# Buffer counts of the gate stage: a second PSUM bank for the gates' matmuls, one bank fewer for transposes, seven one-hot buffers for four

## The chip, the cores and the metric

The kernel runs on one core of one Trainium2 chip. The metric is the device time of one execution in microseconds (us), the median of several runs. Lower is better.

## The reference, cut to what matters

One decoder block over 1024 tokens of width 1024, in float32. A projection feeds sliding-window attention and a short gated convolution; their output is projected, added to the input and normalised (h1). Then comes a mixture of single-neuron experts:

```
q  = h @ w_pq                        # per token 8 heads, two halves of 128
s1, s2 = q[..., :128] @ keys1.T, q[..., 128:] @ keys2.T
v1, i1 = top_k(s1, 16); v2, i2 = top_k(s2, 16)
sc, pos = top_k(v1[:, None] + v2[None, :], 16)
e  = i1[pos // 16] * 128 + i2[pos % 16]   # 16 of 16384 experts per head
g  = softmax(sc)
a  = gelu(u_experts[e] . h)               # 128 experts per token
out = sum_k g * a * v_experts[e]
```

and a second residual and normalisation.

## The kernel before, in words

The 1024 tokens are eight blocks of 128. For the expert stage they are handled in two ways. The blocks 2 to 5 (`DENSE`, L43) are computed densely: every expert's product with every token, by large matmuls, each masked by a gate that is zero for an expert not chosen. The blocks 0, 1, 6 and 7 (`ROWS`, L44) are gathered: for each of the 128 choices of a block, an indirect DMA fetches one row of 1024 floats per token.

**First stage (L207 to L678).** It goes over four groups of two blocks. `project` (L389) does one chunk of 128 output columns: a weight load on SP's queue and eight matmuls into the pool `pm`. The transposes and attention scores, the attention output and the products with the sub keys (L417, L442, L447, L459, L488, L492, L507, L544, L560, L583) all rotate through the pool `pt`, tag `tp`. `keys_of` (L574) takes the top 16 of each head's scores on VectorE. Each `project` also advances two side jobs. One is `side`, the generator `chosen` of the group before (L593), which runs `product_keys` (L301) and, for a dense block, `gates_of_all` (L232). The other is the gathered rows (`advance_rows`, L203).

**The gates (`gates_of_all`).** For eight tokens at a time VectorE builds three one-hot tiles of 128x1024 halfs, `o1` (L280), `oh` and `ol` (L285), all in the tag `hot`, which has four buffers. For each four of these tokens TensorE does eight matmuls (L291, L292) into one tile of the pool `pk`, which is one bank, and ScalarE evicts it in two halves (L295) to the two `st` tiles (tag `st`, two buffers). After 32 tokens both `st` tiles go to memory over SP's queue (L299, 1 MB each). A block is 32 such four-token tiles; the four dense blocks are 128.

**The gathered rows (`all_gathered`, L187).** One generator, in this order: the dot products of block 0 and of block 1 with u rows (`weights_of`, L150, one VectorE instruction a row, L159), the sum of block 0's v rows (`summed_on_pe`, L174), the sum of block 1's (`summed`, L165, one VectorE instruction a row, L170), then blocks 6 and 7 with `weights_of` and `summed`. `summed_on_pe` makes a diagonal tile on ScalarE (L180) and adds the row with two matmuls (L182) into the two banks of the pool `pg`; the profile has four matmul records a row. All rows share five buffers (`NGATHER`), and each gather is issued from POOL's queue (L141).

**Second stage (L681 to L802).** `up` and `down` stream all experts' weights over SP's queue and do the dense matmuls (L709, L741) into a pool of six banks that takes over the banks of `pk`, `pm` and `pt`. Its SBUF tiles too lie where those of the first stage lay. It begins with the reload of h (L691) and reads the gates back (L712). `advance` (L773) places the gathered rows among its units. It ends with `finish` (L754) and the second normalisation.

**Order.** Program order is a priority only: the kernel is built with `schedule_with_timeline_sim=True`, and a planner moves each engine's instructions past each other by its own simulated times and by when buffers come free. On the chip each engine then runs its list in that written order. The matmuls of `summed_on_pe` stand in program order in the second stage and are executed, by the trace, among the last gates of the first.

Of the kernel before, what the change touches and what calls it, by code (L numbers as in the profile page):

```python
# [13 lines left out]
F32 = mybir.dt.float32  # L14
F32R = mybir.dt.float32r
F16 = mybir.dt.float16
# [6 lines left out]
PS = bass.MemoryType.PSUM  # L23
DR = bass.MemoryType.DRAM

P = 128
# [25 lines left out]
OT = 8  # L52
# [25 lines left out]
def block_kernel(ctx: ExitStack, tc: tile.TileContext, d, out):  # L78
# [128 lines left out]
    with ExitStack() as s1:  # L207
        pa = s1.enter_context(tc.tile_pool(name="pa", bufs=1))
        gb = s1.enter_context(tc.tile_pool(name="gb", bufs=1))
        p1 = s1.enter_context(tc.tile_pool(name="p1", bufs=1))  # L210
        p2 = s1.enter_context(tc.tile_pool(name="p2", bufs=1))
        pk = s1.enter_context(tc.tile_pool(name="pk", bufs=1, space=PS))
        pm = s1.enter_context(tc.tile_pool(name="pm", bufs=2, space=PS))
        pt = s1.enter_context(tc.tile_pool(name="pt", bufs=3, space=PS))

        bias = p1.tile([P, 26], F32, name="bias")
        nc.sync.dma_start(bias, d["bias"])
# [14 lines left out]
        def gates_of_all(tb, e1, e2, g):  # L232


            f3 = gb.tile([P, 3, P], F32, name="f3", tag="hot", bufs=4)
            ei = gb.tile([P, P], I32, name="ei")
            V.tensor_copy(f3[:, 0], e1.rearrange("p h k -> p (h k)"))
            V.tensor_copy(ei, e2.rearrange("p h k -> p (h k)"))
            V.tensor_scalar(ei, ei, 7, None, op0=ALU.bitwise_and)
            V.tensor_copy(f3[:, 2], ei)  # L240
            V.tensor_tensor(f3[:, 1], e2.rearrange("p h k -> p (h k)"), f3[:, 2], op=ALU.subtract)
            tp = pk.tile([P, 4, P], F32, name="pk")
            for i in range(3):
                nc.tensor.transpose(tp[:, i], f3[:, i], ident)
            nc.tensor.transpose(tp[:, 3], g.rearrange("p h k -> p (h k)"), ident)
            iT = gb.tile([P, 5, P], F16, name="iT", bufs=2)
            act(iT[:, 0:3], tp[:, 0:3], AF.Copy)
            act(iT[:, 3], tp[:, 3], AF.Copy, scale=GSCALE)
            V.scalar_tensor_tensor(iT[:, 4], tp[:, 3], GSCALE, iT[:, 3], op0=ALU.mult, op1=ALU.subtract)
            i1w = gb.tile([P, P, OT], F16, name="i1w")  # L250
            act(i1w, tp[:, 0, :, None].to_broadcast([P, P, OT]), AF.Copy)

            def wide(o, i, n, step, t0):
                wshp = [P, n, HB // OT, OT]
                V.tensor_tensor(o.rearrange("p n (a t) -> p n a t", t=OT),
                                iT[:, i, t0:t0 + HB].rearrange("p (a t) -> p a t", t=OT)[:, None].to_broadcast(wshp),
                                keys[:, 0:n * step:step, None, :].to_broadcast(wshp), op=ALU.is_equal)

            shp = [P, P, OT]
            shr = [P, OT, P // OT, OT]  # L260
            for t0 in range(0, P, TG):
                if t0 % HB == 0:
                    da = gb.tile([P, 16, HB], F16, name="da")
                    wide(da, 1, 16, 8, t0)
                    db = gb.tile([P, 3, 8, HB], F16, name="db")
                    wide(db[:, 0], 2, 8, 1, t0)
                    for i in (1, 2):
                        V.tensor_tensor(db[:, i], db[:, 0], iT[:, 2 + i, None, t0:t0 + HB].to_broadcast([P, 8, HB]),
                                        op=ALU.mult)
                st = [gb.tile([P, NC // 2, TG], F32, name="st", bufs=2) for _ in range(2)]  # L270
                for t1 in range(t0, t0 + TG, OT):
                    ts = slice(t1, t1 + OT)
                    td = slice(t1 % HB, t1 % HB + OT)

                    def mk(name):
                        return gb.tile(shp, F16, name=name, tag="hot", bufs=4)

                    o1 = gb.tile([P, OT, P], F16, name="o1", tag="hot", bufs=4)
                    oh, ol = mk("oh"), mk("ol")
                    V.tensor_tensor(o1.rearrange("p t (a b) -> p t a b", b=OT),  # L280
                                    i1w[:, ts, None, :].to_broadcast(shr),
                                    row.rearrange("p (a b) -> p a b", b=OT)[:, None].to_broadcast(shr),
                                    op=ALU.is_equal)
                    for o, i in ((oh, 1), (ol, 2)):
                        V.tensor_tensor(o.rearrange("p (a b) t -> p a b t", b=8),  # L285
                                        da[:, :, None, td].to_broadcast([P, 16, 8, OT]),
                                        db[:, i, None, :, td].to_broadcast([P, 16, 8, OT]), op=ALU.mult)
                    for t2 in range(0, OT, 4):
                        ps = pk.tile([P, 4, P], F32, name="pk")
                        for t in range(4):  # L290
                            nc.tensor.matmul(ps[:, t], oh[:, :, t2 + t], o1[:, t2 + t], start=True, stop=False)  # L291
                            nc.tensor.matmul(ps[:, t], ol[:, :, t2 + t], o1[:, t2 + t], start=False, stop=True)  # L292
                        tt = t1 - t0 + t2
                        for z in range(2):
                            act(st[z][:, :, tt:tt + 4].rearrange("p n t -> p t n"),  # L295
                                ps[:, :, z * 64:(z + 1) * 64], AF.Copy, scale=1.0 / GSCALE)
                        yield
                for z in range(2):
                    nc.sync.dma_start(gd[((tb - D0) * P + t0) // TG, :, z * 64:(z + 1) * 64], st[z])  # L299

        def product_keys(tb, v16, i16):  # L301
# [61 lines left out]
            if tb in ROWS:  # L363
                ef = tk.tile([P, NH, TOPK], F32, name="ef")
                V.scalar_tensor_tensor(ef, e1, 128.0, e2, op0=ALU.mult, op1=ALU.add)
                ix = keep.tile([P, NH * TOPK], I32, name=f"ix{tb}")
                V.tensor_copy(ix, ef.rearrange("p h k -> p (h k)"))
                idx[tb] = ix
            else:
                yield from gates_of_all(tb, e1, e2, g)  # L370
# [469 lines left out]
```

## Time and profile before

| | us |
|---|---|
| median of 3 runs | 2766.03 |
| lowest and highest run | 2765.49, 2771.6 |
| the profiled execution | 2761.45 |
| its span, first to last instruction | 2759.6 |
| TensorE matmuls busy | 2476.9 (90%) |
| VectorE busy | 2156.7 (78%) |
| POOL busy | 1378.8 (50%) |
| ScalarE busy | 842.6 (31%) |

The span is cut at about 940 us (last projection), 1225 us (last gate), 1265 us (first dense matmul) and 2665 us (last dense matmul). PE is TensorE, PEld its weight load, DVE VectorE, ACT ScalarE; SPq is SP's DMA queue. A busy PE is not PE at its peak, since ends of matmuls are modelled.

### The profile page before, as it was taken

The page shows a single profiled execution, that of the slowest core. Times are in us where ns is not written, and L with a number is a line of the kernel's source. Part 1 is how long each engine was busy: PE and PEld are TensorE (multiplying, and loading weights), DVE is VectorE, ACT ScalarE, POOL GpSimd, SP SyncE. Part 2 cuts the span into 40 slices and gives each one's busy share as a digit, 9 for nine tenths or more (in the row PEclk, how much of TensorE's full clock was granted, in tenths as well). Part 3 has the DMA queues.
Part 4 walks back from the last instruction along what each step waited for, and adds up shares of the span by engine and source line. Part 5 has one row for each costly group of instructions (what it writes and reads, how often), then busy time and mean ns, then how long its engine had stood idle before and what let it go on. Part 6 is the DMA issues. An engine that isn't in the chain of part 4 may idle for free. (4 is left out here: it accounts for less than half of the span.)

```text
span 2759.6 us, 34442 instructions
## 1 busy us (share of the span) xinstructions
PE 2476.9 (90%) x11544; PEld 1992.3 (72%) x11544; DVE 2156.7 (78%) x4829; ACT 842.6 (31%) x1434; POOL 1378.8 (50%) x1233
## 2 busy tenths in 40 slices
PE   8999699779876999966999999999999999999960
PEld 7888588668765744435888888888888888888850
DVE  2158889999999844238888788888888888888898
ACT  2123122242433444343323332232322323232211
POOL 1001533443343244435666666666676666766663
PEclk9899799789977999987999999999999999999985
DMA  6345999899989588889999999999999999999997
GB/s 202 98 156 182 353 376 336 311 360 338 342 322 321 173 298 300 293 284 345 342 348 334 339 358 335 357 333 350 340 341 347 340 346 339 346 352 337 339 317 270
DMA packets 293905, 862.29 MB, mean 312 GB/s; under 512 B 25824, under 2 KB 97760, under 8 KB 289504
## 3 DMA queue, kind: packets, MB, share of 16 engines
q0 software_dynamic: 150480, 548.47, 54.4%
q1 hardware_dynamic: 143248, 311.62, 32.8%
q8 instruction: 91, 1.49, 0.2%
q14 instruction: 86, 0.70, 0.1%
HBM read 815.95 MB, written 44.04 MB: 312 GB/s over the span
## 5 line engine op out<-in xcount | busy, mean ns | idle before, releaser
L141 POOL DMA_INDIRECT row<-in_u,ix x512 | 526.0, 1027 | 625.0 <-DVE row L159 234.9
L141 POOL DMA_INDIRECT row<-in_v,ix x512 | 525.9, 1027 | 486.5 <-PE pg L182 199.9
L709 PE MATMUL pd<-hT,uh 128*128 128x512 f32 x2048 | 635.0, 390 | 41.5 <-ACT uh L120 41.5
L159 DVE SCALAR_TENSOR_TENSOR row<-row,pg 128x1024 f32<-128x1024 f32 x512 | 613.8, 1212 | 37.7 <-DMA row<-in_u,ix 33.1
L170 DVE SCALAR_TENSOR_TENSOR pg<-row,a,pg 128x1024 f32<-128x1024 f32 x384 | 493.3, 1285 | 38.4 <-DMA row<-in_v,ix 34.2
L709 PEld LDWEIGHTS pd<-hT,uh 128*128 128x128 f32 x2048 | 385.6, 188 | 121.7 <-ACT uh L120 41.7
L741 PE MATMUL pd<-Wl,vh 128*128 128x512 f32 (+1 forms) x1056 | 403.1, 383 | 0.2 <-DVE Wl L121 0.2
L709 PE MATMUL pd<-hT,ul 128*128 128x512 f32 x1024 | 399.5, 390 | 0.0
L741 PE MATMUL pd<-Wh,vh 128*128 128x512 f32 (+1 forms) x1056 | 396.9, 383 | 0.1
L741 PE MATMUL pd<-Wh,vl 128*128 128x512 f32 (+1 forms) x1056 | 392.6, 383 | 0.0
L121 POOL TENSOR_TENSOR vl<-vraw,vh 128x1024 fp32r<-128x1024 f32 x128 | 308.8, 2412 | 69.2 <-ACT vh L120 65.4
L394 PE MATMUL mm<-x,raw 128*128 128x256 f32 x1152 | 268.6, 386 | 12.6 <-DMA x<-in_xT 7.8
L120 ACT ACTIVATE vh<-vraw 128x1024 fp32r<-128x1024 f32 x128 | 135.9, 1062 | 466.2 <-PE pd L741 302.6
L747 DVE TENSOR_TENSOR accT<-accT,pd 128x512 f32<-128x512 f32 (+1 forms) x256 | 169.2, 667 | 106.6 <-PE pd L741 99.5
L182 PE MATMUL pg<-row,dg 128*128 128x512 f32 x512 | 238.7, 606 | 14.3 <-ACT dg L180 11.0
L394 PEld LDWEIGHTS mm<-x,raw 128*128 128x128 f32 x1152 | 216.3, 193 | 43.5 <-issue 7.9
L394 PE MATMUL mm<-h,raw 128*128 128x256 f32 x1024 | 236.1, 382 | 0.6 <-ACT h L563 0.6
L741 PEld LDWEIGHTS pd<-Wl,vh 128*128 128x128 f32 x1056 | 198.3, 188 | 39.0 <-DVE Wl L121 0.4
L741 PEld LDWEIGHTS pd<-Wh,vl 128*128 128x128 f32 x1056 | 198.4, 188 | 38.9 <-POOL vl L121 0.2
L741 PEld LDWEIGHTS pd<-Wh,vh 128*128 128x128 f32 x1056 | 198.0, 188 | 39.0 <-issue 0.3
L709 PEld LDWEIGHTS pd<-hT,ul 128*128 128x128 f32 x1024 | 192.8, 188 | 40.9 <-DVE ul L121 0.8
L121 DVE TENSOR_TENSOR ul<-uraw,uh 128x1024 fp32r<-128x1024 f32 x128 | 159.1, 1243 | 70.5 <-ACT uh L120 65.3
(214 smaller groups left out, 2955.7 us busy)
## 6 DMA issues: line engine op xcount, KB each, us to landing
raw<-in_wall SPq DMA_DIRECT2D x168, 512.0 KB
uraw<-in_uT SPq DMA_DIRECT2D x128, 512.0 KB
vraw<-in_vL SPq DMA_DIRECT2D x128, 512.0 KB
gd<-st SPq DMA_DIRECT2D x32, 1024.0 KB
gq<-gd SPq DMA_DIRECT2D x32, 1024.0 KB
row<-in_u,ix POOLq DMA_INDIRECT x512
row<-in_v,ix POOLq DMA_INDIRECT x512
x<-in_xT SPq DMA_DIRECT2D x16, 256.0 KB
```

The source lines that it names most:

```text
L120: act(dh, src, AF.Copy)
L121: eng.tensor_tensor(dl, src, dh.bitcast(F32), op=ALU.subtract)
L141: G.indirect_dma_start(out=row, out_offset=None, in_=d[table], in_offset=bass.IndirectOffsetOnAxis(ap=idx[tb][:, k:k + 1], axis=0))
L159: V.scalar_tensor_tensor(row, row, 1.0, h1p, op0=ALU.mult, op1=ALU.mult, accum_out=a[:, k:k + 1])
L170: V.scalar_tensor_tensor(acc, rows_of(tb, "v", k), a[:, k:k + 1], acc, op0=ALU.mult, op1=ALU.add)
L182: nc.tensor.matmul(acc[:, z:z + 512], dg, row[:, z:z + 512], start=(k == 0), stop=(k == P - 1))
L394: nc.tensor.matmul(ps[:, :n], w[:, j], mov[:, j, :n], start=(j == 0), stop=(j == NJ - 1))
L709: nc.tensor.matmul(ps, w[:, j], hT[z][:, j], start=(j == 0 and k == 0), stop=(j == NJ - 1 and k == 2))
L741: nc.tensor.matmul(ps, vv[:, j % 2, k], w[:, t0:t0 + n], start=(k == 0 and p == 0), stop=(k == QUAD - 1 and p == 2))
L747: V.tensor_tensor(o, o, ps, op=ALU.add)
```

## The change

It changes four numbers of buffers and nothing else. The pool `pk` gets a second bank, `pt` goes from three banks to two (with two of `pm` and two of `pg` the sum stays eight), and the tag `hot` goes from four to seven buffers of 2 KB a partition, in all three places that use it. No instruction is added, removed or given another shape; `summed_on_pe` is the same in both kernels. The planner works out the order of every engine anew.

```diff
-        pk = s1.enter_context(tc.tile_pool(name="pk", bufs=1, space=PS))
+        pk = s1.enter_context(tc.tile_pool(name="pk", bufs=2, space=PS))
         pm = s1.enter_context(tc.tile_pool(name="pm", bufs=2, space=PS))
-        pt = s1.enter_context(tc.tile_pool(name="pt", bufs=3, space=PS))
+        pt = s1.enter_context(tc.tile_pool(name="pt", bufs=2, space=PS))
...
-            f3 = gb.tile([P, 3, P], F32, name="f3", tag="hot", bufs=4)
+            f3 = gb.tile([P, 3, P], F32, name="f3", tag="hot", bufs=7)
...
                     def mk(name):
-                        return gb.tile(shp, F16, name=name, tag="hot", bufs=4)
-
-                    o1 = gb.tile([P, OT, P], F16, name="o1", tag="hot", bufs=4)
+                        return gb.tile(shp, F16, name=name, tag="hot", bufs=7)
+
+                    o1 = gb.tile([P, OT, P], F16, name="o1", tag="hot", bufs=7)
```

## Rows read from the trace of the kernel before

**Rows 1.** The page's 40 slices of 69 us, busy tenths.
```profile
PE   8999699779876999966999999999999999999960
DVE  2158889999999844238888788888888888888898
DMA  6345999899989588889999999999999999999997
```
**Rows 2.** Windows of all engines: busy us (records), then clock, DMA share, GB/s.
```profile
core 0: us, PE busy (x) PEld busy (x) DVE busy (x) ACT busy (x) POOL busy (x), PEclk, DMA share, GB/s
...
570.00:940.00 370.00, 305.55 (x1754) 261.14 (x1753) 353.92 (x1232) 130.05 (x276) 128.16 (x125) 0.86 0.85 309
940.00:1225.00 285.00, 257.75 (x1016) 128.49 (x1014) 120.20 (x392) 128.37 (x272) 126.22 (x128) 0.98 0.83 286
1225.00:1265.00 40.00, 0.00 (x0) 0.00 (x0) 19.09 (x16) 4.96 (x6) 14.55 (x16) 0.50 1.04 372
...
1300.00:2600.00 1300.00, 1300.00 (x5737) 1076.35 (x5736) 1097.78 (x1408) 405.30 (x506) 863.20 (x670) 1.00 0.96 344
```
**Rows 3.** Timeline of 1000 to 1012 us, all engines.
```profile
1001.64 0.22 PE L291 MATMUL pk<-o,oh 128*128 128x128 f16 x1
...
1002.13 3.65 PE L182 MATMUL pg<-row,dg 128*128 128x512 f32 x8
1002.27 0.69 DVE L285 TENSOR_TENSOR oh<-da,db 128x1024 f16<-128x1024 f16 x1 [6.08 <-PE pk L291]
1002.34 1.05 ACT L295 ACTIVATE st<-pk 128x256 f32<-128x256 f32 x2
...
1005.62 0.22 PE L291 MATMUL pk<-o,oh 128*128 128x128 f16 x1
```
**Rows 4.** Waits in 940 to 1225 us: us in total, times, longest.
```profile
DVE oh L285 <- PE pk L291: 159.7, 25, 12.2
POOL row L141 <- PE pg L182: 140.4, 117, 4.4
...
ACT st L295 <- DMA gd<-st: 41.3, 12, 4.9
...
PE pk L291 <- ACT st L295: 10.0, 9, 1.5
```
**Rows 5.** Timelines of SP's queue (970 to 1015 us) and ScalarE (1009 to 1024 us).
```profile
976.19 35.56 SPq L299 DMA_DIRECT2D gd<-st  x4
...
1022.40 0.60 ACT L295 ACTIVATE st<-pk 128x256 f32<-128x256 f32 x1 [2.56 <-DMA gd<-st]
```
**Rows 6.** Timelines of SP's queue and TensorE around the change of stage.
```profile
1225.47 5.17 SPq L691 DMA_DIRECT2D hr<-hTd  x4
...
1265.42 1.22 PE L709 MATMUL pd<-hT,uh 128*128 128x512 f32 x2 [41.47 <-ACT uh L120]
```
**Rows 7.** VectorE's row sums L170: one window, and the group after 2665 us.
```profile
1300.00:1550.00 250.00, 132.27 (x103) 1.00 0.96 343
...
L170 DVE SCALAR_TENSOR_TENSOR pg<-row,a,pg 128x1024 f32<-128x1024 f32 x46 | 59.3, 1289 | 9.3 <-DMA row<-in_v,ix 8.2
```
**Rows 8.** First attention block's window, the instructions on its banks, who waits for tile tp.
```profile
45.00:75.00 30.00, 30.00 (x163) 26.24 (x162) 7.84 (x23) 9.14 (x29) 0.00 (x0) 1.00 0.60 194
...
L471 DVE TENSOR_REDUCE nm<-sp x32: 415/677/692, 45.3 to 761.9; 128x2 f32<-128x512 f32 x28, 128x2 f32<-128x256 f32 x4
...
L476 ACT ACTIVATE S<-sp,nm x64: 357/472/502, 48.1 to 768.4; 128x256 f32<-128x256 f32 x56, 128x128 f32<-128x128 f32 x8
...
L496 ACT ACTIVATE pT<-tp x32: 383/597/671, 54.9 to 774.8; 128x512 f32<-128x512 f32 x28, 128x256 f32<-128x256 f32 x4
...
  DVE v L220: 33.7, 20
```
**Rows 9.** Timeline of POOL, 860 to 960 us: the longest pause of the gather.
```profile
926.36 0.94 POOL L141 DMA_INDIRECT row<-in_v,ix  x1 [49.92 <-PE pg L182]
```

## The prediction

> **What bounds the kernel now.** I read the slices first. PE is nearly full from about 940 us to the end, but VectorE is the full one before that, and the DMA share dips twice, at 900 and towards 1200 us [rows 1]. So there are stages, and I cut the span into windows. From 570 to 940 us VectorE is busy 353.9 of 370 us: it is the bound there. From 1300 to 2600 us PE is busy without a gap and the DMA engines stand at 0.96 and 344 GB/s: both are full [rows 2]. In between lies the stretch that the change is about, 940 to 1225 us, with the gates of blocks 4 and 5 (64 tiles of four tokens) and 124 of block 0's 128 rows; VectorE is busy only 120.2 of its 285 us and the DMA engines move 286 GB/s [rows 2]. The second stage waits for its end: the reload of h is issued at 1225.47 us, and PE then does nothing for 41.5 us [rows 6].
>
> The waits of that stretch say what paces it. VectorE waits 159.7 us for the gates' matmuls to free a one-hot buffer; ScalarE waits 41.3 us for an `st` buffer; but PE waits only 10.0 us for an eviction of its one bank [rows 4]. The timeline shows the beat: a tile's matmuls begin at 1001.64 us and the next tile's at 1005.62, that is 3.98 us, of which 0.49 us is the tile and 3.49 us are two rows (1.75 us each) that stand between them in PE's list; the next one-hot tile starts only behind the first tile [rows 3]. So a chain of buffers paces the gates, and PE fills the gaps with rows.
>
> The end has a second condition. When the dense matmuls stop at 2665 us, 46 rows are still to be added; that takes 46 x 1.48 us, to 2733 us (the rows themselves take 1.289 us), and 27 us of normalisation follow. In the second stage the rows come at 103 in 250 us, 2.43 us each [rows 7]. Check of that model: 384 rows by 1225 us and 1440 us / 2.43 = 593 by 2665 us make 977; the trace has 978.
>
> **The change, part by part.** No instruction changes, so every term is a wait or an order.
>
> *Seven one-hot buffers and the second bank.* Two sets of three tiles fit beside each other, so VectorE builds one set while PE reads the other, and an eviction no longer stops the next tile. The new beat is not in the trace. From below it is ScalarE's 1.05 us for two evictions [rows 3] (or VectorE's 120.2 us for the whole stretch, if that binds), from above the 3.98 us of now. I take one row between two tiles instead of two, 1.75 + 0.49 = 2.24 us, since PE's list has the rows ready and a row, once begun, isn't interrupted. Then `st` is next: it keeps two buffers. Four issues of it in 35.56 us are two pairs, 34.8 us apart, for eight tiles; the second pair is issued at about 1011 us and ScalarE gets its second buffer back at 1022.4, so 11.4 us later [rows 5]. One us of that is covered by the next tile, so eight tiles now cost 8 x 2.24 + 10.4 = 28.3 us instead of 34.8. Eight such sets save 8 x 6.5 = 52 us: the last gate comes at 1173 us. With both edges, between 1060 us (VectorE's work alone) and 1225 us.
>
> A rule speaks against the bank. The row says that PE waits 10.0 us for it in this stretch [rows 4]. The Trainium skill (TensorE: Matmul & The Clock Gate, section "HAM oscillation — how this bites in real kernels") tells of a matmul kernel in which PSUM double-buffering brought no further gain. By the row the bank is worth at most its 10 us and the rest is the one-hot buffers'; by that rule the sum below would lose those 10 us and be 2749 us.
>
> *What PE does with it.* In the 285 - 52 = 233 us up to 1173 us PE spends 64 x 0.49 = 31 us on tiles and has 202 us for rows: 115 of 124. The 9 left take 16 us, and they lie in the 41.5 us hole in which PE had nothing [rows 6]: no cost. The dense matmuls keep their 1400 us, so PE's end moves by the whole 52 us, to 2613 us.
>
> *What the rows do with it.* At 1173 us 260 + 115 = 375 rows are done. 1440 us at 2.43 us give 593 more: 968 at PE's end, 56 left, 56 x 1.48 = 83 us, so 2696 us instead of 2733: 37 us sooner. The gain shrinks from 52 to 37 us, since the first stage hands over fewer finished rows.
>
> *One bank fewer in `pt`.* Attention now has two banks where it had three. For each of 8 blocks the second pair of score tiles must wait for a reduce and two exponentials, 0.68 + 2 x 0.47 = 1.6 us; the transposes of the probabilities, 3 of 4 tiles a block, each wait for a copy of 0.60 us and its transposes, about 0.9 us [rows 8]. At most 8 x 1.6 + 24 x 1.0 = 37 us, if nothing covers it; at least nothing, as in the first attention block, where PE is busy 30 of 30 us with projections between [rows 8]. I take 10 us: four blocks lie in the stretch before 300 us, where PE is nearly full and a stall counts; the others lie where VectorE is the bound.
>
> *The first half of the gates, 570 to 940 us.* Nothing: VectorE has no room there [rows 2]; a gate that goes earlier pushes another instruction out. If that cover is wrong it is rival three. *The 6 KB more of SBUF:* nothing; it only decides which old tile the second stage lies on.
>
> Sum: -37 + 10 = -27 us on the profiled execution's 2761.45 us, 2734.5 us. That execution lies 4.6 us under the median of 2766.03 us; on the median the forecast is 2739 us.
>
> **The rivals.**
>
> *One: too early or not at all (2760 to 2766 us).* If the gates run at VectorE's pace, the last comes at 1060 us and only 51 rows are done by then. PE then carries 56 rows of 1.75 us (98 us) among dense matmuls, beyond the 17 that fit into the hole, and ends at 1060 + 41 + 1400 + 98 = 2599 us; 80 rows are left, 118 us, so 2717 us: 16 us sooner, 6 with `pt`'s loss, 2760 us. Or the planner keeps two rows between tiles and nothing moves: 2766 us. For it: VectorE is idle for 165 us of the stretch. Against: `st` has still two buffers.
>
> *Two: the lost bank decides (2800 us).* The key products use `pt` too, and each tile is held by the top-16 chains of two blocks. VectorE waits 33.7 us now for these products [rows 8]. If the third bank is what kept that low, the wait doubles: 34 us. With attention's whole 37 us that makes 71 us, less 37 us gained: 34 us slower, 2800 us. It decides from a loss of 37 us on. For it: PE runs its list in order, so each wait for a bank stops the projections. Against: the projections between already cover much, and VectorE is the bound after 300 us.
>
> *Three: the pause closes too (2708 us).* From about 876 to 926 us the gather stands still for 49.9 us, waiting for PE to add the first rows, while the planner put projections and gates ahead [rows 9]. If the new order lets the gather go on, 50 / 2.43 = 21 more rows come before the end, 21 x 1.48 = 31 us: 2708 us. For it: the gates behind would no longer need PE's slots late. Against: nothing in the diff names these rows.
>
> *Four: the bank is worth nothing.* Then the 10 us of its waits stay and the time is 2749 us; it still counts as faster. The Trainium skill's section named above is this rival's rule.
>
> **How the numbers follow.** A measurement of this kernel can tell about 0.2% (5.5 us) from no change. The forecast has 0.42, rival four 0.08, rival three 0.14: faster 0.64. Rival one has 0.13, nearly all within 0.2%. Slower has 0.23: rival two in part or whole, from 2772 us on. The predicted time is the likeliest, 2739 us; its own range is 2717 to 2757 us, from `pt` at nothing with some of the pause closed, to `pt` at 28 us. The range of 2700 to 2785 us takes in rival three and half of rival two, and leaves out about 2 in 10.
>
> **What would show it.** Right: the wait of `oh` for the gates' matmuls falls from 159.7 us to under 60; the reload of h is issued near 1173 us (1130 to 1200); PE's idle time before L709 is filled in part by L182; L741 ends near 2613 us with 50 to 60 rows left. ScalarE's wait for `st` grows from 41.3 us. Wrong: the reload still at 1225 us (the planner kept its order); or the last projection well behind 940 us (the lost bank); or L709 waiting behind L182 for rows.

## The result: 5.5% slower, and the profile after

The changed kernel takes 2921.04 us (2915.81 to 2923.12) against 2766.03: a ratio of 1.055, 95% interval 1.052 to 1.058. The prediction said 2739 us and 2700 to 2785: wrong in sign and outside its range. The profiled execution of after takes 2915.81 us, its span 2914.0 us; before's span was 2759.6 us, so 154.4 us have to be found.

First the page's slices of after, 73 us each, to be held against [rows 1].

```profile
PE   9898799678859997999999999999999999994000
DVE  2159899999997793221158888888888888888888
DMA  6246999889987578466679999999999999999997
```

Two things differ. In the low stretch of VectorE, now slices 16 to 20, the DMA share is 4 to 6 in the last four slices; before, it was 8 throughout that stretch. And PE stops three and a half slices before the end, where before it stopped one and a half before.

The windows of all engines put numbers on that (columns as in [rows 2]); the second fence is a window of before that was not shown, for the same columns.

```profile
core 0: us, PE busy (x) PEld busy (x) DVE busy (x) ACT busy (x) POOL busy (x), PEclk, DMA share, GB/s
0.00:1087.90 1087.90, 930.97 (x4934) 766.81 (x4935) 856.97 (x3162) 351.50 (x780) 318.16 (x367) 0.90 0.76 272
...
1087.00:1129.00 42.00, 23.61 (x50) 9.34 (x48) 15.98 (x40) 11.14 (x19) 14.69 (x13) 0.84 1.03 372
1129.00:1483.00 354.00, 353.71 (x1289) 243.35 (x1290) 80.22 (x97) 104.24 (x169) 119.93 (x93) 0.99 0.58 186
1600.00:2653.00 1053.00, 1053.00 (x4745) 876.37 (x4744) 898.28 (x1186) 320.00 (x398) 705.21 (x549) 1.00 0.95 343
2653.00:2890.00 237.00, 2.37 (x20) 1.89 (x18) 198.62 (x190) 3.02 (x5) 141.90 (x153) 0.51 0.95 344
```
```profile
0.00:1225.50 1225.50, 1075.53 (x5272) 828.77 (x5272) 871.43 (x3205) 395.50 (x871) 397.87 (x455) 0.91 0.79 279
```

Next, three rows of after, each on one line of the kernel: the reload of h; all matmuls of block 0's rows, and their weight loads up to the reload (times are lowest/median/highest in ns, then first and last start).

```profile
L691 SPq DMA_DIRECT2D hr<-hTd x4: 1208/1323/1557, 1087.9 to 1092.0; - x4
...
L182 PE MATMUL pg<-row,dg x512: 590/592/1191, 884.2 to 1483.3; 128*128 128x512 f32 x171
...
L182 PEld LDWEIGHTS pg<-row,dg x175: 186/190/197, 884.0 to 1087.9; 128*128 128x128 f32 x175
```

**The first stage ends 138 us sooner, and has done that much less.** The reload comes at 1087.9 us, before at 1225.47 [rows 6]. But PE has been busy for 931.0 us by then, against 1075.5: 144.6 us less. Its idle time up to the reload did not fall; it went from 150 to 157 us. What was left out are rows: of 512 weight loads (four a row) 175 are done, 44 rows of 128, while before all 128 were done by 1214 us. 84 rows x 1.75 us are 147 us.

**Those rows go on in the second stage, at half the pace.** Eleven more run before the dense matmuls begin at 1129 us, and 73 among them, until 1483 us: 354 / 73 = 4.85 us a row, where rows came at 2.43 us before [rows 7]. One generator makes all rows in turn, through five buffers, and nothing behind block 0 passes it in the trace: block 1's first sum starts at 1495 us. In those 354 us PE is full, VectorE is busy for 80 us and the DMA engines stand at 0.58 and 186 GB/s. The waits of this stretch (us in total, times, longest) name it, and the timeline of PE shows the rows between dense matmuls.

```profile
ACT dg L180 <- PE pg L182: 137.5, 68, 5.0
POOL row L141 <- PE pg L182: 124.0, 49, 9.9
```
```profile
1301.24 1.88 PE L182 MATMUL pg<-row,dg 128*128 128x512 f32 x4
1302.55 0.80 PE L741 MATMUL pd<-Wh,vl 128*128 128x512 f32 x1
...
1306.38 1.88 PE L182 MATMUL pg<-row,dg 128*128 128x512 f32 x4
...
1308.56 1.88 PE L182 MATMUL pg<-row,dg 128*128 128x512 f32 x4
...
1313.70 1.88 PE L182 MATMUL pg<-row,dg 128*128 128x512 f32 x4
```

ScalarE's next diagonal and POOL's next gather both wait for a row's matmuls, and these wait for their place in PE's list.

**The rest is paid at the end.** After 1483 us the old pace is back: 486 rows in the 1170 us up to 2653, 2.41 us each. There the dense matmuls end, 12 us sooner than before, for PE has the same work to do in all. But 154 rows are left, where 46 were. The groups of the last stretch, 2653 us to the end (busy, mean ns, then idle before and releasers):

```profile
L170 DVE SCALAR_TENSOR_TENSOR pg<-row,a,pg 128x1024 f32<-128x1024 f32 x128 | 165.1, 1290 | 30.6 <-DMA row<-in_v,ix 27.4 <-DVE pg L170 0.2
L159 DVE SCALAR_TENSOR_TENSOR row<-row,pg 128x1024 f32<-128x1024 f32 x26 | 31.7, 1220 | 6.6 <-DMA row<-in_u,ix 6.1
```

They take 233 us, to 2886, which is 1.51 us each, with PE idle and the DMA share at 0.95; 27 us of normalisation follow. The balance: 108 more rows x 1.5 us = 162 us, less the 12, is 150 us of the 154. Of these rows 73 are the slow stretch's own: 354 us at 2.43 would have held 146 rows and held 73, which is 110 us at the end. So in this kernel

    span = last dense matmul + 1.5 us x rows then left + 27 us

For after it gives 2911 (measured 2914.0), for before 2761 (2759.6). The experiments are read by it.

### The profile page after: what moved, and what is told of

It reads as the page before. It is cut to its first block, busy times and chain, and to the rows that moved or that the text cites. A ratio compares the mean times of both kernels' runs of the same rounds, so it can differ in the third digit from the quotient of the medians.

```text
span 2914.0 us, 34443 instructions
## 1 busy us (share of the span) xinstructions
PE 2479.8 (85%) x11544; PEld 1993.9 (68%) x11544; DVE 2168.0 (74%) x4829; ACT 838.4 (29%) x1436; POOL 1375.6 (47%) x1233
## 5 line engine op out<-in xcount | busy, mean ns | idle before, releaser
L709 PE MATMUL pd<-hT,uh 128*128 128x512 f32 x2048 | 642.6, 393 | 13.9 <-ACT uh L120 13.9
L170 DVE SCALAR_TENSOR_TENSOR pg<-row,a,pg 128x1024 f32<-128x1024 f32 x384 | 493.7, 1286 | 40.2 <-DMA row<-in_v,ix 35.1
L741 PE MATMUL pd<-Wh,vl 128*128 128x512 f32 (+1 forms) x1056 | 398.9, 388 | 0.0
L182 PE MATMUL pg<-row,dg 128*128 128x512 f32 x512 | 241.1, 601 | 10.2 <-DMA row<-in_v,ix 8.1
```

The costliest lines, as they stand in the source:

```text
L170: V.scalar_tensor_tensor(acc, rows_of(tb, "v", k), a[:, k:k + 1], acc, op0=ALU.mult, op1=ALU.add)
L182: nc.tensor.matmul(acc[:, z:z + 512], dg, row[:, z:z + 512], start=(k == 0), stop=(k == P - 1))
L709: nc.tensor.matmul(ps, w[:, j], hT[z][:, j], start=(j == 0 and k == 0), stop=(j == NJ - 1 and k == 2))
L741: nc.tensor.matmul(ps, vv[:, j % 2, k], w[:, t0:t0 + n], start=(k == 0 and p == 0), stop=(k == QUAD - 1 and p == 2))
```

## The experiments

Theory A is what stands above: with the new buffers the planner puts more gates and fewer rows into PE's list of the first stage, and the rows left for the second stage need the one engine that is full there. The runs and their law (us; "rows left" at the last dense matmul; before's medians beside them were 2764.24 to 2767.15):

| run | median | ratio (95%) | reload | last dense | rows left | law | span |
|---|---|---|---|---|---|---|---|
| before | 2766.03 | | 1225.5 | 2665 | 46 | 2761 | 2759.6 |
| after | 2921.04 | 1.055 (1.052 to 1.058) | 1087.9 | 2653 | 154 | 2911 | 2914.0 |
| e1_pt_two | 2788.50 | 1.009 (1.007 to 1.0109) | 1254.5 | 2701.5 | 36 | 2782 | 2781.8 |
| e2_hot_seven | 2814.09 | 1.0168 (1.0149 to 1.0186) | 1183.5 | 2639 | 95 | 2808 | 2812.4 |
| e3_bank_two | 2907.79 | 1.0517 (1.05 to 1.0535) | 1089.3 | 2644 | 153 | 2900 | 2905.8 |
| e4_rows_first | 2867.14 | 1.0363 (1.0344 to 1.0383) | 1089.3 | 2656 | 120 | 2863 | 2865.9 |
| e5_after_dve | 2745.35 | 0.9914 (0.9895 to 0.9932) | 1077.3 | 2535 | 122 | 2745 | 2747.6 |
| e6_before_dve | 2757.68 | 0.9964 (0.9952 to 0.9977) | 1175.2 | 2618 | 73 | 2755 | 2756.1 |
| e8_hot_rows | 2764.51 | 0.9997 (0.9984 to 1.001) | 1182.5 | 2635 | 64 | 2758 | 2758.7 |
| e9_hold | 2782.83 | 1.0052 (1.0033 to 1.0071) | 1245.3 | 2665 | 51 | 2768 | 2770.0 |
| e10_dg | 2913.86 | 1.0531 (1.0513 to 1.0548) | 1116.0 | 2670 | 144 | 2913 | 2918.3 |
| e11_hot_dve | 2754.11 | 0.9953 (0.9936 to 0.997) | 1092.6 | 2544 | 119 | 2749 | 2752.6 |
| e12_pm_one | 2761.29 | 0.998 (0.9967 to 0.9992) | 1076.0 | 2535 | 135 | 2764 | 2768.7 |
| e13_split | 2762.29 | 0.9979 (0.9969 to 0.999) | 1088.8 | 2533 | 132 | 2758 | 2762.1 |

(Law and span are of the profiled execution; for e9_hold the reload's last part is given.)

### The change in its parts

**e1_pt_two**: the lost bank alone.

```diff
-        pt = s1.enter_context(tc.tile_pool(name="pt", bufs=3, space=PS))
+        pt = s1.enter_context(tc.tile_pool(name="pt", bufs=2, space=PS))
```

> The kernel before with the pool pt at two banks, one-hot buffers at four, pk at one. Theory A (the rows of block 0 that need TensorE are left over in the second stage): the gates' beat stays 4 us a tile, the reload of h stays near 1225 us, block 0's matmul rows end before it, 40 to 60 rows are left when the dense matmuls end; time 2755 to 2800 us. Theory B (the lost bank of pt is the cause): first-stage projections end near 1026 us as in the changed kernel, instead of 935, and the time is 2870 us or more.

2788.5 us, +24 on the median, in theory A's range: the lost bank costs, but it is not the 155. The reload comes 29 us later, where A had it unmoved, and the copies of the key projections end at 970.7 us, where before's end at 935.0.

**e2_hot_seven**: the seven one-hot buffers alone (`bufs=4` to `7` in the three places).

> The kernel before with seven one-hot buffers alone, pt at three banks, pk at one. Theory A: most of the earlier end of the gates comes from these buffers, so the reload comes by 1150 us, at least 40 rows of block 0 fall into the second stage at some 4.8 us each, and the time is 2840 to 2920 us. Theory B: pt is whole, so the time is 2725 to 2770 us.

Neither theory's range: 2814 us. The direction is A's, but the reload comes 42 us sooner and not 75, with 110 of 128 rows done by then. Twelve more run before the first dense matmul. The last six (24 matmul records) drag on to 1319 us all the same; a window of all engines shows what that does.

```profile
1225.10:1319.40 94.30, 94.26 (x388) 73.61 (x389) 31.18 (x33) 36.50 (x51) 20.33 (x12) 0.98 0.45 147
```

PE is full, and VectorE and the gather are nearly still. It is the state of after, for 94 us in place of 354, and for six rows in place of 73: 15.7 us a row. So a full PE does not by itself make 4.85 us a row; where the planner puts the rows in PE's list does.

**e3_bank_two**: the second bank of `pk` with `pt` at two; the one-hot buffers stay four.

```diff
-        pk = s1.enter_context(tc.tile_pool(name="pk", bufs=1, space=PS))
+        pk = s1.enter_context(tc.tile_pool(name="pk", bufs=2, space=PS))
-        pt = s1.enter_context(tc.tile_pool(name="pt", bufs=3, space=PS))
+        pt = s1.enter_context(tc.tile_pool(name="pt", bufs=2, space=PS))
```

> The kernel before with the second bank of pk and two banks of pt, one-hot buffers at four. Theory A: the one-hot buffers still pace the gates, VectorE still waits over 100 us for L291 in their stretch, the reload comes after 1180 us, time 2750 to 2810 us. Theory B: as the changed kernel, 2870 us or more.

A miss for theory A, which laid the gates' pace to the one-hot buffers; the time is theory B's, though e1 shows that the lost bank is not the cause. e3 and e1 differ in the second bank of `pk` alone, and it brings nearly all: the reload at 1089 us where e1 has 1254, and 2908 us where e1 has 2788. (The second bank beside three of `pt` would be a ninth; it was not run.) The window up to the reload of e1, then of e3:

```profile
0.00:1254.50 1254.50, 1081.28 (x5272) 827.63 (x5272) 882.44 (x3212) 399.38 (x871) 405.57 (x464) 0.91 0.77 276
```
```profile
0.00:1089.30 1089.30, 943.66 (x4969) 767.80 (x4970) 864.15 (x3194) 357.49 (x791) 324.94 (x375) 0.91 0.76 276
```

Of the 165 us, 138 are work of PE that was not done. How the list looks in e3, from PE's timeline (of each group of small matmuls only the first entry is shown: 16 matmuls, two tiles, in e3; 8, one tile, in e2), and how in e2:

```profile
1039.58 3.17 PE L182 MATMUL pg<-row,dg 128*128 128x512 f32 x7
1042.58 0.29 PE L291 MATMUL pk<-o,oh 128*128 128x128 f16 x2
...
1043.57 3.65 PE L182 MATMUL pg<-row,dg 128*128 128x512 f32 x8
```
```profile
1059.76 3.65 PE L182 MATMUL pg<-row,dg 128*128 128x512 f32 x8
1063.25 0.22 PE L291 MATMUL pk<-o,oh 128*128 128x128 f16 x1
...
1063.74 3.65 PE L182 MATMUL pg<-row,dg 128*128 128x512 f32 x8
1067.23 0.22 PE L291 MATMUL pk<-o,oh 128*128 128x128 f16 x1
```

With one bank the list has two rows (eight records) behind every tile, as before [rows 3]; with two banks, behind every second tile. So half the rows find a place between these tiles; over the whole run 52 of 128 rows are done by e3's reload (209 of 512 matmul records).

### Rows first, or rows off PE

**e4_rows_first**: after, with block 0's rows ahead of the second stage in program order, which is their priority.

```diff
+        while done < 3 * P:
+            step()
```

> The changed kernel with the gathered rows up to the end of block 0's sum put in program order before the second stage. Theory A: block 0's matmul rows then have priority over the dense matmuls, they end by 1260 us at 2.0 to 2.5 us a row, 40 to 70 rows are left at the end of the dense matmuls; time 2700 to 2770 us, 150 us or more below the changed kernel. Theory B: nothing changes in the first stage, so the time stays 2880 us or more.

Right in direction, a miss in size: 2867 us, between the two theories. 43 rows are done by the reload (174 weight loads), as in after, and the last ends at 1400 us instead of 1483: 3.7 us a row. The 83 us that this saves are 34 rows at 2.43 us, and 34 rows fewer are left. Priority shortens the queue and does not undo it.

**e5_after_dve** and **e6_before_dve**: after, and before, with block 0 summed on VectorE.

```diff
-        yield from summed_on_pe(ROWS[0], a0)
+        yield from summed(ROWS[0], a0)
```

> The changed kernel with block 0's rows summed by VectorE (summed instead of summed_on_pe), nothing else. Theory A (an early second stage harms only because block 0's rows then queue in TensorE's full list): with no row on TensorE the gather keeps 2.4 us a row from the start of the second stage, near 1090 to 1130 us, the dense matmuls end near 2500 us, and the time is 2700 to 2810 us, at least 110 below the changed kernel. Theory C (the gather is slow early in the second stage whatever engine adds the rows, since the dense loads take the DMA or POOL): rows still come at over 4 us each up to some 1480 us, time over 2870 us.

> The kernel before with block 0's rows summed by VectorE. Theory A: TensorE loses 224 us of row matmuls, the gates' beat falls below 4 us a tile, as no rows stand between the tiles; with the gather the bound behind it, 2720 to 2800 us. Theory C: as the kernel before, 2750 to 2800 us. This run is the partner of the one above: it says what the buffers alone are worth without rows on TensorE.

Both as theory A had it; e6's time lies in theory C's range too, so only e5 tells the two apart. With the rows off PE the very same buffers make the kernel faster, by 0.4%: 2745.35 us (2743.66 to 2749.70) against 2757.68 (2754.37 to 2767.28) for the four old numbers, and against 2766.5 for before. The windows of e5, all engines:

```profile
940.00:1114.40 174.40, 110.91 (x725) 95.87 (x725) 167.12 (x463) 63.67 (x126) 71.16 (x57) 0.76 0.88 313
1114.40:2535.20 1420.80, 1407.36 (x6255) 1164.57 (x6256) 1228.24 (x1700) 448.17 (x560) 950.94 (x717) 0.99 0.94 335
```

The slow stretch is gone: from the first dense matmul on 319 sums and 256 dot products, 575 rows, come in 1420.8 us, 2.47 us each, at a DMA share of 0.94. The rival that laid the loss to the early start of the second stage itself falls with it: the reload comes at 1077 us here, sooner than in after.

**e8_hot_rows**: seven one-hot buffers, one bank in `pk`, three in `pt`, and the loop of e4.

> The kernel before with seven one-hot buffers alone (pt three banks, pk one) and the gathered rows up to the end of block 0's sum in program order before the second stage. Theory A: the six rows that were left over in the run with seven buffers alone now end by 1240 us instead of 1319, 30 to 60 rows are left at the end of the dense matmuls, time 2710 to 2770 us. If the planner's order of these rows doesn't matter: 2800 to 2820 us as without it.

Theory A's time, with a few us and rows more than it said: the same reload as e2 (1182.5 us) and the same 110 rows by then, but the others end at 1247.5 us instead of 1319. e2 and e8 differ in the rows' priority alone, so this pair is the cleanest on the order of the list. The last six rows, among dense matmuls, in e2 and then in e8 (busy us and records of PE's matmuls on L182, then of their weight loads; then clock, DMA share, GB/s of the stretch):

```profile
1225.10:1319.40 94.30, 11.71 (x24) 5.12 (x24) 0.98 0.45 147
```
```profile
1223.40:1247.80 24.40, 12.70 (x24) 5.11 (x24) 0.91 0.64 210
```

The same matmuls take 24 us in place of 94. At 2.43 us a row the 70 us are 29 rows; 64 rows are left instead of 95, and 50 us come back. Against before nothing is won: 0.9997.

**e9_hold**: e4, and the second stage's first tile reads a word of block 0's result, so that no dense matmul can start before block 0 is done.

```diff
+        finals[tb] = o
...
+        while done < 3 * P + 1:
+            step()
...
+            if j == 0:
+                V.tensor_copy(hr[:, 0, 0:1], finals[ROWS[0]][:, 0:1])
```

> The changed kernel with the rows first as in the earlier run, and the second stage held back by a data dependency: its first reload of h may only start when block 0's finished output stands (one element of it is copied into the reload's buffer first). Theory A: the second stage starts some 150 to 200 us later than in the changed kernel, its dense matmuls end near 2700 to 2720 us, but only 40 to 60 rows are left then: 2780 to 2830 us, about 100 below the changed kernel although its second stage starts later. Theory C or any theory by which an earlier second stage is worth something: 2950 us or more.

Theory A's time, and the plainest of the runs: TensorE's dense work begins 129 us later than in after, and the kernel is 138 us faster (84 us faster than e4, which has the same priority and no hold). The dense work began and ended somewhat sooner than A said, at 1258 and 2665 us. Block 0's matmuls, then the first dense product's, of e9 (lines moved by the edit):

```profile
L185 PE MATMUL pg<-row,dg x512: 592/592/1057, 879.3 to 1236.5; 128*128 128x512 f32 x171
```
```profile
L717 PE MATMUL pd<-hT,uh x2048: 389/389/796, 1258.2 to 2638.7; 128*128 128x512 f32 x187
```

### What else could hold the rows, and what the buffers are worth

**e10_dg**: after, with four diagonal tiles for two. ScalarE's wait for a diagonal's buffer is the longest that touches the rows, so theory D held that the count of diagonals makes 4.85 us.

```diff
-            dg = gp.tile([P, P], F32, name="dg", bufs=2)
+            dg = gp.tile([P, P], F32, name="dg", bufs=4)
```

> The changed kernel with four diagonal tiles for two. In it each row left over in the second stage took 4.85 us, and ScalarE waited over 130 us there for L182 to free a diagonal. Theory D (the two diagonals and ScalarE's list set that 4.85 us): rows go at under 3.5 us, they end by 1390 us, time under 2880 us. Theory A (TensorE's list, full of dense matmuls, sets it): rows still end near 1450 to 1500 us, time 2900 to 2930 us.

D falls. ScalarE's wait drops from 137.5 us (1129 to 1483 us of after) to 63.4 (1130 to 1480 us here), and the rows still end at 1477 us. 63 rows run there from the first dense matmul at 1158.8 us on, 5.05 us each:

```profile
L182 PE MATMUL pg<-row,dg x512: 591/592/1167, 882.0 to 1476.9; 128*128 128x512 f32 x171
...
ACT dg L180 <- PE pg L182: 63.4, 56, 3.1
```

**e11_hot_dve**: e5 with one bank in `pk` and three in `pt`, so of the change only the one-hot buffers.

> Seven one-hot buffers alone, pt at three banks, pk at one, and block 0's rows summed by VectorE. By theory A the time is the end of the dense matmuls plus 1.5 us for each row left plus 27 us. The third bank of pt is worth some 20 us here, the missing second bank of pk costs a later gate: reload near 1120 to 1170 us, 2735 to 2765 us.

2754.11 us, in the range; the reload, at 1092.6 us, comes sooner than expected. With rows off PE, e6 to e11 to e5 is 2757.7, 2754.1, 2745.35. The intervals of e6 and e11 overlap, so a gain by the one-hot buffers alone is not shown; that of e5 lies below both.

**e12_pm_one**: e5, but the bank for `pk` is taken from `pm` (two to one) and `pt` keeps its three.

> The changed kernel with block 0's rows summed by VectorE, and the bank for pk taken from pm (one bank) instead of pt (three). If pt's bank was worth the 25 us that its loss cost alone, and pm's costs less: 2715 to 2740 us. If pm's bank is worth more, since every projection then waits for the eviction of the one before: 2760 to 2830 us.

The second case: 2761.29 us, 16 slower than e5. The bank of `pm` is worth more than that of `pt`. The reload and the last dense matmul come when they do in e5, but 313 rows are done at the first dense matmul (1110.6 us), where e5 has 330 (1114.4 us). Why is not shown. ScalarE waits longer for the key projections' matmuls, 179.0 us by 1110 us, than in e5 (124.4), but before waits 165.3 us there with two banks:

```profile
ACT cT L582 <- PE mm L394: 179.0, 46, 4.6
```

**e13_split**: after, with the first 48 rows of block 0 on PE and 80 on VectorE, so that PE's rows end with the first stage.

```diff
+            if k >= 48:
+                V.scalar_tensor_tensor(acc, row, a[:, k:k + 1], acc, op0=ALU.mult, op1=ALU.add)
+                yield True
+                continue
```

> The changed kernel with the first 48 rows of block 0 added by TensorE and the other 80 by VectorE into the same PSUM tile, so that no row needs TensorE in the second stage and VectorE, busy 167 of 174 us before it in the run that sums all 128 there, is relieved. Theory A: some 15 to 25 more rows by the start of the second stage, time 2705 to 2745 us, below both kernels. If TensorE's rows cost elsewhere what they save: 2745 us or more.

The second case: 2762.29 us, not under e5. PE's rows do end before the first dense matmul, at 1102 us, but the split is no better than all rows on VectorE: 312 rows are done at the first dense matmul (1130 us), where e5 has 330 at 1114 us. The dense matmuls end at 2533 us here and at 2535 in e5, and 132 rows are left, there 122.

The fastest version found is e5: 2745.35 us, 0.9914 of before, less than 1%.

## Why the prediction was wrong, step by step

**What bounds the kernel now**: the three stages, the idle time before the first dense matmul (for the kernel before) and the end's second condition held. The law above is that condition.

**Seven one-hot buffers and the second bank**: half right. VectorE's wait for a one-hot buffer fell as forecast, from 159.7 us to 17.1 (in after's 940 to 1087 us). The beat of 2.24 us a tile is the new list's: two tiles and two rows in 4.47 us (in after, from 1040.13 to 1044.60 us). But the pause of 10.4 us in eight tiles for `st` did not come (23.7 us of such waits in after's 940 to 1087 us, 41.3 before [rows 4]), and the gates ended at 1087 us, not at 1173. The parts were dealt wrongly too: 10 us to the bank from its wait. A wait shows what the chip waited for in a list in which the planner had already put rows under the evictions [rows 3]; what the bank allows the planner to write is no wait. The Trainium skill (TensorE: Matmul & The Clock Gate, section "HAM oscillation — how this bites in real kernels") reports of one matmul kernel that PSUM double-buffering brought it no further gain. Here the second bank moved the reload, by 165 us from e1 to e3, and brought no gain in time either: it cost 119 us.

**What PE does with it**: the right question, mis-sized. The step counts 31 us of tiles and 217 us of rows and leaves out 10 us of other work: PE was busy for 257.75 of these 285 us [rows 2], so at most 27 us could be won by closing gaps. A stage that ends 52 us sooner has to hand over the difference, 14 rows and not 9. One that ends 138 us sooner handed over 84: 11 of them ran in the hole, and 73 did not fit. PE's end moved by 12 us, not by 52.

**What the rows do with it** is the step that failed most: "1440 us at 2.43 us". That pace was measured while the rows' sums ran on VectorE, which had room. The rows handed over are PE's, and PE is full in the second stage; they came at 4.85 us for 354 us, with every later row behind them. The step had no term for a row that waits in PE's list, since its 9 rows all fell into the hole. In the step's own terms, 311 rows at the first dense matmul, 73 (not 146) to 1483 and 486 to 2653 make 870 of 1024. The step's pace would have left 81 rows and 2802 us, which is slower than before by the handing over alone; the pace adds the other 110.

**One bank fewer in `pt`**: 0 to 37 us, 10 taken; e1 measures 24. The range held, the place did not: up to 300 us, where the step laid the cost, PE is busy for 268.7 us in e1 and 269.8 in before, but from 300 to 570 us for 225.5 against 242.4. VectorE's wait for the key products, which went into rival two, hardly grew: 36.3 us in e1, 33.7 before [rows 8].

**The first half of the gates**: taken as nothing; 159 evictions are done by 940 us in after, where 129 were, so 15 of the 64 tiles of the later stretch went earlier, while the last key projections moved from 935 to 1027 us. The other 49 took 147 us, 3.0 us each, where the step above had 28.3 / 8 = 3.5. At that price the 15 tiles are 53 of the 86 us between 1173 and 1087.

**The rivals.** One had the place right (gates near 1060 us, rows left for PE) and the sign wrong: it priced the rows at PE's 1.75 us each and let the others run on at 2.43. Two was a real cost of a smaller size (24 us, where it had 71 before the gain) and from another place. Three came in part and won nothing: the pause of 49.9 us is gone and after has done 12 rows by 940 us, before 3, but pauses of 34.3 and 25.9 us follow. Four falls with e3. No rival had a loss of 155 us.

**Still open**: why PE's list spaces the left rows 4.85 us apart (15.7 in e2; 3.7 and 4.0 with priority, in e4 and e8) when it could have put them closer. The planner writes the list by its own simulated times, which no run here shows; the number of diagonal tiles is excluded.

## What to carry to other kernels

Before a stage with side work in it is shortened, read how busy its fullest engine is: only its idle time can be won, and what goes beyond that is side work pushed into the next stage. Then ask which engine that work needs there; if it is that stage's bound, its old pace doesn't hold, and everything in the same queue waits with it, for as long as the list's order says. A buffer's worth in a planned instruction list is not read from the wait for it, since the planner has filled that wait with other work: 10 us of waits here stood for a bank that moved the stage's end by 165 us.

## What was not expected of the hardware

In e6, where PE has little to do among the gates, its granted clock fell to 0.51 of full speed, the lower of its two levels, and a gate matmul took 311 ns in the median where the timelines above show 0.22 us beside rows. The window of all engines, and the gates' matmuls over the run:

```profile
940.00:1217.50 277.50, 77.62 (x533) 60.38 (x532) 245.65 (x575) 87.36 (x154) 130.35 (x97) 0.51 0.77 273
```
```profile
L291 PE MATMUL pk<-o,oh x512: 217/311/332, 564.5 to 1173.2; 128*128 128x128 f16 x171
```

The kernel was faster than before all the same (0.9964): PE is busy for 78 of these 277.5 us, and VectorE, at 246, is the full one. What the low clock cost here, no run separates; the engine had 200 us of room in this stretch.
